# A hybrid decoder layer on one core: a narrow attention block as three fp32r matmuls, one FFN block's tiles loaded ahead, two heads' sums later

## The chip, the core and the metric

One NeuronCore of a Trainium2 chip. The time is that of the whole launch on the device in microseconds (us), the median of several runs. Five engines work side by side and meet through semaphores: TensorE (PE in the rows; its weight loads are PEld), VectorE (DVE), ScalarE (ACT), GpSimd (POOL) and SyncE (SP). SP and POOL also issue most of the DMAs, each in the order of its own queue.

## What is computed

512 tokens with 16 meta tokens ahead of them (L = 528), width 2048, one layer, all in float32. Cut to what matters:

```python
n = _rmsnorm(h, g_mix);  p = n @ w_in            # q | k | v for 8 heads of 128, and gb | gc | u
z = q @ k.T / sqrt(128)                          # q and k normed per head
log_beta, log_keep = log_sigmoid(z), where(causal, log_sigmoid(-z), 0)
log_pass = cumsum(log_keep, reverse=True) - log_keep
w = where(causal, exp(log_beta + log_pass), 0);  o_attn = w @ v
o_conv = gb * causal_dwconv3(gc * u)
h = h + concat(rmsnorm(o_attn), rmsnorm(o_conv)) @ w_out
h = h + (silu(n2 @ w_gate) * (n2 @ w_up)) @ w_down   # n2 = rmsnorm(h), hidden width 5632
```

## The kernel before

**Numbers in two parts.** Each fp32 product is made of three fp32r matmuls: a number is split into a high part (a cast to fp32r) and a low part (the number less that), and hi x hi, hi x lo and lo x hi are added in PSUM. `split` does it: `sc.copy` (ACT) writes the high part, a `tensor_tensor` (DVE) the low one. Weights stream in through SP's DMAs into `w_buf` and are split by `split_quad` (L188, L189) into `s_buf`. TensorE works through one long series of such products; everything else is fitted in between.

**The order of the work around it.** The projections go head by head: `product` runs over the 16 k tiles of the input for k (`pk`), q (`pq`) and v (`pv`). After each k tile, `tick()` counts down the pieces of work that `after(n, work)` has put on a list, and calls what is due; so `after(6, ...)` places a piece six k tiles later in the program. A scheduler then sets each engine's order from the program and its own priorities; it may move an instruction a little, as `order` rows below show. A k tile of `pk` or `pv` is six matmuls of 264 columns, one of `pq` or `pb` three of 512, one of `pcu` six of 260.

**One head's attention.** `attend` (due some k tiles after `pv`) transposes v with TensorE (L521, L522), splits it into `vh`, `vl`, and makes the logits z in three PSUM tiles. The 1344 columns of `lw`, `sp`, `lb` are the causal blocks of 128 keys: `SEG` cuts them into three segments, s = 2, 1, 0. Segment 2 holds three key blocks: 272 columns for keys 256 to 383, 144 columns for keys 384 to 511, and 16 columns for the last 16 keys. `sums(2)`, `sums(1)`, `sums(0)` (L596, L597 for s below 2) make the reverse cumulative sums with a triangular matrix; each passes the first row on to the next segment, through a one-row add (L602) and a split of that row, whose low part is the `spl` that L597 reads. Then `exp`, the causal mask (POOL, L554), and a split into `wh`, `wl`. `mix` multiplies the weights with the values into `o`: three fp32r matmuls for each of the 512, 400 and 272 columns (L621 to L623), and plain fp32 matmuls for the 144 columns (L624, values in `v32[:, :P]`) and the 16 columns (L625, 16 rows). Heads 1 to 6 have their work behind the next head's projections; head 7 has it behind the first convolution products `pcu` and `pb`.

**The FFN's input blocks.** The FFN products use seven blocks of activations for four products' worth of work (a Strassen-like scheme): `acts[0..6]`, each with a high and a low part and 8 k tiles. Blocks 3, 4 and 6 are written to DRAM (`fx`) tile by tile while the output projection runs, and loaded back at its end, when the memory of the projection's operands is free. Tile 7 is made last and written straight to SBUF. `pair_product` runs the blocks in the order 5, 0, 1, 2, 3, 4, 6 for the first pair; its matmuls are L753, and a block takes high activations with high weights, low activations with high weights, then high with low weights, 8 tiles each.

Of the kernel before, what the change touches and what calls it, by code (L numbers as in the profile page):

```python
# [9 lines left out]
F32 = mybir.dt.float32  # L10
F32R = mybir.dt.float32r
# [4 lines left out]
P = 128  # L16
D = 2048
SEQ = 512
META = 16
L = META + SEQ  # L20
HEADS = 8
# [8 lines left out]
Q0 = [0, 112, 240, 368, 496]  # L30
# [3 lines left out]
def hybrid_layer(ctx: ExitStack, tc: tile.TileContext, xT, w_in, w_out, w_gu, w_down, vecs, out):  # L34
# [10 lines left out]
    ve, sc, gp, pe = nc.vector, nc.scalar, nc.gpsimd, nc.tensor  # L45
# [108 lines left out]
    quads, sums, split_w, used, loaded = {}, {}, [], [0], [0]  # L154
# [111 lines left out]
    def after(k_tiles, work):  # L266
        waiting.append([k_tiles, work])
# [31 lines left out]
    def split(hi, lo, src, eng=ve, turn=False):  # L299
        in_order(sc.copy(hi, src), turn)  # L300
        eng.tensor_tensor(lo, src, hi.bitcast(F32), ALU.subtract)  # L301
# [187 lines left out]
    def head(h):  # L489

        if h:
            pk = pp.tile([P, 2, 512], F32, tag="pp", name=f"pk{h}")
            product([(pk[:, 0, :H], 0, H), (pk[:, 1, :H], H, L)], n_hl)
        else:
            pk = pk0
        kn = kns[0]
        kh = apool.tile([P, 384], F32R, tag="kh", name=f"kh{h}")
        kl = apool.tile([P, 384], F32R, tag="kl", name=f"kl{h}")
        after(8 if h else 11, qk_norm(halves(pk, H), g_k, L, kn[:, :L], (kh, kl, 384), f"k{h}"))

        if h:
            pq = pp.tile([P, 2, 512], F32, tag="pp", name=f"pq{h}")
            product([(pq[:, 0, :], META, L)], n_hl)
        else:
            pq = pq0
        qn = apool.tile([P, SEQ], F32, tag="qn", name=f"qn{h}")
        qh = apool.tile([P, SEQ], F32R, tag="qh", name=f"qh{h}")
        ql = apool.tile([P, SEQ], F32R, tag="ql", name=f"ql{h}")
        after(9 if h else 12, qk_norm(pq[:, 0, :], gq_s, SEQ, qn, (qh, ql, SEQ), f"q{h}"))

        pv = pp.tile([P, 2, 512], F32, tag="pp", name=f"pv{h}")
        product([(pv[:, 0, :H], 0, H), (pv[:, 1, :H], H, L)], n_hl)
        vt = t512(L, "e", 2)
        ve.tensor_tensor(two(vt[:, :L]), halves(pv, H), two(r), ALU.mult)
        after(6 if h else 11, lambda: attend(h, kn, kh, kl, qn, qh, ql, vt))

    def attend(h, kn, kh, kl, qn, qh, ql, vt):

# [1 line left out]
        for b in range(4):  # L520
            pe.transpose(ta[:, b * P : (b + 1) * P], vt[:, b * P : (b + 1) * P], ident)  # L521
        pe.transpose(tb[:16, :P], vt[:, 512:L], ident)  # L522
        vh = apool.tile([P, 384], F32R, tag="vh", name=f"vh{h}")
        vl = apool.tile([P, 384], F32R, tag="vl", name=f"vl{h}")
        v32 = apool.tile([P, 256], F32, tag="v32", name=f"v32{h}")
        split(vh, vl, ta[:, :384])
        ve.tensor_copy(v32[:, :P], ta[:, 384:512])
        ve.tensor_copy(v32[:16, P:], tb[:16, :P])


        zs = []
# [24 lines left out]
                    base=base, channel_multiplier=-1,  # L556
                )

        hl, ws = [None] * 3, [None] * 3
        for s in (2, 1, 0):  # L560
            a, b = SEG[s]
            z = zs[s][:, : b - a]
# [23 lines left out]
        def sums(s):  # L586
            a, b = SEG[s]
            th, tl = hl[s]
            c = small(f"c{h}_{s}")
            if s == 2:  # L590
                pe.matmul(c[:, :432], later_r, th, start=True, stop=False)
                pe.matmul(c[:, :432], later_r, tl, start=False, stop=False)
                pe.matmul(c[:, P:416], ones_r, bh, start=False, stop=False)
                pe.matmul(c[:, P:416], ones_r, bl, start=False, stop=True)
            else:
                pe.matmul(c[:, : b - a], carry, th, start=True, stop=False)  # L596
                pe.matmul(c[:, : b - a], carry, tl, start=False, stop=True)  # L597
            if s:

                n, (a0, b0) = SEQ - Q0[s], SEG[s - 1]  # L600
                th, tl = hl[s - 1]
                ve.tensor_tensor(lw[0:1, b0 - n : b0], c[0:1, :n], sp[0:1, a : a + n], ALU.add)  # L602
                split(th[0:1, :], tl[0:1, :], lw[0:1, a0:b0])
                after(6, lambda: sums(s - 1))
            ve.tensor_tensor(lb[:, a:b], lb[:, a:b], c[:, : b - a], ALU.subtract)
            sc.activation(lw[:, a:b], lb[:, a:b], AF.Exp)
            causal(lw, s)
            n = (512, 400, 272)[s]
            th = apool.tile([P, b - a], F32R, tag=f"th{s}", name=f"wh{h}_{s}")
            tl = apool.tile([P, b - a], F32R, tag=f"tl{s}", name=f"wl{h}_{s}")  # L610
            split(th[:, :n], tl[:, :n], lw[:, a : a + n])
            ws[s] = (th[:, :n], tl[:, :n])
            if s == 0:
                after(11, lambda: mix(ws))

        def mix(ws):
            o = small(f"o{h}")
            for b in range(3):
                kk, q0 = slice(b * P, (b + 1) * P), Q0[b]
                th, tl = ws[b]  # L620
                pe.matmul(o[:, q0:], vh[:, kk], th, start=b == 0, stop=False)  # L621
                pe.matmul(o[:, q0:], vh[:, kk], tl, start=False, stop=False)
                pe.matmul(o[:, q0:], vl[:, kk], th, start=False, stop=False)  # L623
            pe.matmul(o[:, Q0[3] :], v32[:, :P], lw[:, 1184:1328], start=False, stop=False)  # L624
            pe.matmul(o[:, Q0[4] :], v32[:16, P:], lw[:16, 1328:1344], start=False, stop=True)  # L625
            g = g_att[:, h : h + 1]
            oh, ol, store = stage_out(f"a{h}")
            sc.activation(oh, o, AF.Copy, scale=g)
            ve.scalar_tensor_tensor(ol, o, g, oh.bitcast(F32), ALU.mult, ALU.subtract)
            store()  # L630
            square_sum(acc_a, o, h == 0)
# [290 lines left out]
    for i, j in enumerate(OUT_TILES):  # L922
# [35 lines left out]
        if i == KT - 1:  # L958
            with tc.high_priority(1 << 20):
                residual(ve)  # L960
                mixed_blocks()
                square_sum(acc_h, hj, False, wide_tmp("s"), ve)
            oapool.release()
            oc2_pool.release()
            ocpool.release()
            accpool.release()
            fp = open_pool("fp")
            sides = fp.tile([P, 3 * T2], F32, name="sides")
            rings_p = {0: open_pool("ring_0")}
            pad(rings_p[0], 32)  # L970
            rings, n_ring, ring = {}, [6], {}

            groups = {0: (0, 1), 1: (1, 2), 3: (1, 1), 4: (1, 1), 5: (1, 1), 6: (2, 1), 7: (2, 5)}

            def new_places(i):
                p, m = groups[i]
                for n, t in enumerate(slots(rings_p[p], F32R, m, 6, f"ring{i}", tail=4 if i == 7 else 60, tag=f"ring{i}")):
                    ring[i + n] = t

            def ring_place():  # L980
                n_ring[0] += 1
                return ring[(n_ring[0] - 1) % 12]

            new_places(0)
            fpool_4 = open_pool("fpool_4")
            acts[4] = slot(fpool_4, F32R, 8, "f4", "f4")
            gu_pool = open_pool("gu_pool")
            gu = [gu_pool.tile([P, 2, T2], F32, name=f"gu{m}") for m in range(2)]
            pad(gu_pool, 768)
            fpool_last = open_pool("fpool_last")  # L990
            acts[3] = slot(fpool_last, F32R, 8, "f3", "f3")
            acts[6] = slot(fpool_last, F32R, 8, "f6", "f6", tail=4)
            for s, n in ((3, 6), (6, 7)):
                for part in range(2):
                    nc.sync.dma_start(acts[s][:, part, :n].bitcast(F32), fx[s][:, part, :n].bitcast(F32), max_dma_last_dim=4096)
            gp.dma_start(acts[3][:, :, 6], fx[3][:, :, 6])
            for part in range(2):
                gp.dma_start(acts[4][:, part, :7], fx[4][:, part, :7], max_dma_last_dim=4096)
            split_f(3, 6)
            split_f(4, 7)  # L1000
            split_f(6, 3)
        else:
            residual(gp if half and i < KT - 2 else ve)
            if half:
                split_f(5, 2)
                if i < KT - 2:
                    st = hbuf.tile([P, 2, 2, T2], F32R, tag="st", name=f"st{j}")[:, :, 0]
                    split(st[:, 0], st[:, 1], src[:, 3])
                    gp.dma_start(fx[6][:, :, k], st)
            else:  # L1010
                mixed_blocks()
                st = hbuf.tile([P, 2, 2, T2], F32R, tag="st", name=f"st{j}")
                split(st[:, 0], st[:, 1], src[:, 6:8])
                for n, s in enumerate((3, 4)):
                    gp.dma_start(fx[s][:, :, k], st[:, :, n])
# [241 lines left out]
```

## Time and profile before

| | |
|---|---|
| median of 3 runs | 2035.27 us (2034.88 to 2036.73) |
| the profiled execution | 2035.44 us, span 2033.7 us |
| granted TensorE clock | 1.00 |
| matmul records | 16158 |
| busy: PE, DVE, ACT, POOL | 2025.3, 1721.2, 1050.1, 382.1 us |
| HBM | 278.50 MB read, 80.61 MB written |

The timeline has a start, a duration, the engine, the line, the operation with out<-in, and in square brackets the idle time of the engine ahead of it with what ended it. Matmuls overlap, so the distance from one start to the next is what one costs. A list of waits has the waiting instruction, the one waited for, then the microseconds in total, the number of times and the longest. A plain fp32 matmul is two records, an fp32r matmul one. Rows by tile have counts and the least, median and largest duration in ns.

### The profile page before, as it was taken

What the parts mean: (1) busy time and instruction counts of PE and PEld (TensorE: products, weight loads), DVE (VectorE), ACT (ScalarE), POOL (GpSimd) and SP (SyncE); (2) the same over time, 40 slices, a digit from 0 to 9 for tenths busy, and PEclk for the clock granted to TensorE, in tenths of its full rate; (3) what the DMA queues carried; (4) which work ended last, traced back from release to release, by engine and by line L of the source; (5) the groups of instructions that cost most, each with busy time, mean ns of one, the idle gap of its engine ahead of it and who ended that gap; (6) DMA issues with size and microseconds to landing.
All of it is one profiled execution on the core that took longest, in us unless ns stands there. A gap on an engine that the chain in (4) does not pass through costs nothing.

```text
span 2033.7 us, 39736 instructions
## 1 busy us (share of the span) xinstructions
PE 2025.3 (100%) x16158; PEld 1964.0 (97%) x16158; DVE 1721.2 (85%) x2202; ACT 1050.1 (52%) x1517; POOL 382.1 (19%) x531
## 2 busy tenths in 40 slices
PE   9999999999999999999999999999999999999999
PEld 8999999999998889999999999999999999999999
DVE  8788878588877679998998998988989898888887
ACT  7666666444443435554554555555555544444443
POOL 0111111220015440111110110110110242222111
PEclk9999999999999999999999999999999999999999
DMA  6333344753365656556555555555555999989864
GB/s 231 106 125 116 124 139 133 253 153 106 104 212 181 188 173 231 167 160 181 159 160 160 160 161 158 161 161 157 164 159 156 288 322 294 244 234 265 231 149 89
DMA packets 162007, 361.70 MB, mean 178 GB/s; under 512 B 13600, under 2 KB 73760, under 8 KB 161824
## 3 DMA queue, kind: packets, MB, share of 16 engines
q1 hardware_dynamic: 79744, 229.47, 35.4%
q0 software_dynamic: 81936, 129.65, 24.3%
q8 instruction: 127, 2.08, 0.4%
q14 instruction: 56, 0.46, 0.1%
q10 hardware_dynamic: 144, 0.04, 0.0%
HBM read 278.50 MB, written 80.61 MB: 177 GB/s over the span
## 4 chain that ended last, share of the span: by engine, by line
PE 96%; DVE 1%; DMA 1%; ACT 1%; issue 0%; POOL 0%; SPq 0%; DVEq 0%; ACTq 0%
PE x L753 40%; PE z L753 20%; PE y L753 10%; PE po L859 3%; PE po L860 3%; PE po L861 3%; PE pv L286 1%; PE pv L288 1%; PE pv L290 1%; PE pk L286 1%; PE pk L288 1%; PE pk L290 1%; PE pq L290 1%; PE pq L286 1%; PE pq L288 1%; PE pcu L286 1%
## 5 line engine op out<-in xcount | busy, mean ns | idle before, releaser
L188 ACT CAST s_buf<-w_buf 128x1024 fp32r<-128x1024 f32 (+2 forms) x665 | 659.5, 992 | 755.2 <-PE x L753 368.8
L189 DVE TENSOR_TENSOR s_buf<-w_buf,s_buf 128x1024 fp32r<-128x1024 f32 (+2 forms) x665 | 767.1, 1154 | 123.3 <-ACT s_buf L188 121.4
L753 PE MATMUL x<-f,s_buf 128*128 128x256 f32 x4224 | 500.6, 275 | 1.0 <-DMA f<-fx 1.0
L753 PEld LDWEIGHTS x<-f,s_buf 128*128 128x128 f32 x4224 | 488.9, 188 | 1.3 <-DMA f<-fx 1.2
L207 DVE TENSOR_TENSOR w_buf<-w_buf 128x1024 f32<-128x1024 f32 (+1 forms) x243 | 278.3, 1145 | 16.7 <-DMA w_buf<-w_in 10.0
L753 PE MATMUL z<-f,s_buf 128*128 128x256 f32 x2112 | 253.6, 275 | 0.0
L753 PEld LDWEIGHTS z<-f,s_buf 128*128 128x128 f32 x2112 | 245.9, 188 | 0.0
L1054 POOL DMA_DIRECT2D fd<-s x147 | 103.9, 923 | 701.2 <-DVE s L301 700.0
L753 PE MATMUL x<-ring,s_buf 128*128 128x256 f32 x1824 | 219.2, 275 | 0.0
L753 PEld LDWEIGHTS x<-ring,s_buf 128*128 128x128 f32 x1824 | 212.4, 188 | 0.0
L753 PE MATMUL y<-f,s_buf 128*128 128x256 f32 x1056 | 126.8, 275 | 0.0
L753 PEld LDWEIGHTS y<-f,s_buf 128*128 128x128 f32 x1056 | 123.1, 188 | 0.1
L1127 POOL DMA_DIRECT2D out_T<-d x62 | 60.7, 1014 | 284.9 <-DVE d L1135 206.7
L753 PE MATMUL z<-ring,s_buf 128*128 128x256 f32 x864 | 105.7, 275 | 0.0
L753 PEld LDWEIGHTS z<-ring,s_buf 128*128 128x128 f32 x864 | 101.5, 188 | 0.0
L225 DVE TENSOR_TENSOR w_buf<-w_buf 128x1024 f32<-128x1024 f32 (+1 forms) x81 | 92.3, 1139 | 1.4 <-DMA w_buf<-w_down 1.4
L753 PE MATMUL x<-nh,s_buf 128*128 128x260 f32 x432 | 59.3, 282 | 0.0
L753 PEld LDWEIGHTS x<-nh,s_buf 128*128 128x128 f32 x432 | 55.0, 188 | 0.1
L789 DVE SCALAR_TENSOR_TENSOR gu<-z,sides 128x256 f32<-128x256 f32 x44 | 18.7, 425 | 42.7 <-PE z L753 42.6
L753 PE MATMUL z<-blk,s_buf 128*128 128x260 f32 x432 | 54.8, 282 | 0.0
L286 PE MATMUL pk<-nh,s_buf 128*128 128x264 f32 x256 | 52.9, 288 | 0.9 <-ACT nh L357 0.8
L753 PEld LDWEIGHTS z<-blk,s_buf 128*128 128x128 f32 x432 | 53.1, 188 | 0.0
(344 smaller groups left out, 3320.5 us busy)
## 6 DMA issues: line engine op xcount, KB each, us to landing
w_buf<-w_gu SPq DMA_DIRECT2D x176, 512.0 KB, 3.5
w_buf<-w_in SPq DMA_DIRECT2D x92, 512.0 KB, 3.4
fd<-s POOLq DMA_DIRECT2D x147, 256.0 KB, 5.2
w_buf<-w_down SPq DMA_DIRECT2D x96, 384.0 KB, 5.0
ring<-fd POOLq DMA_DIRECT2D x42, 768.0 KB, 9.2
w_buf<-w_out SPq DMA_DIRECT2D x32, 512.0 KB, 3.5
out_T<-d POOLq DMA_DIRECT2D x62, 256.0 KB, 5.5
fc<-st SPq DMA_DIRECT2D x8, 1040.0 KB, 6.1
```

The costliest lines, as they stand in the source:

```text
L188: sc.copy(hi, src)
L189: in_turn(ve.tensor_tensor(lo, src, hi.bitcast(F32), ALU.subtract), turn)
L207: in_turn(ve.tensor_tensor(sums[name], a, b, ALU.add), turn)
L225: ve.tensor_tensor(sums["t2"], sums["t2"], b["21"], ALU.add)
L286: pe.matmul(ps, wh, ah[:, a:b], start=k == 0, stop=False)
L288: pe.matmul(ps, wh, al[:, a:b], start=False, stop=False)
L290: pe.matmul(ps, wl, ah[:, a:b], start=False, stop=k == last)
L753: pe.matmul(p, wt[:, kk], act(part, k), start=first, stop=wt is lo and k == n - 1, skip_group_check=skip)
L859: pe.matmul(ps, hi[:, kk], ah, start=k == order[0], stop=False)
L860: pe.matmul(ps, hi[:, kk], al, start=False, stop=False)
L861: pe.matmul(ps, lo[:, kk], ah, start=False, stop=k == order[-1])
L1054: gp.dma_start(fd[c][s][:, :, k], t[:, :, i])
```

## The change

It has three parts. The 144 columns of segment 2 are multiplied as three fp32r matmuls: the values of all 512 keys are split, `v32` keeps only the last 16 keys, and the 144 columns of weights are split as well, one segment later, into free columns of segment 2's tiles. The loads of FFN block 4 are written ahead for its first six tiles, and tile 6 of blocks 3 and 4 comes behind them. And in heads 0 and 7 each `sums` stands seven k tiles behind the one before, not six; head 0's `attend` stands 12 behind, not 11.

```diff
-        after(6 if h else 11, lambda: attend(h, kn, kh, kl, qn, qh, ql, vt))
+        after(6 if h else 12, lambda: attend(h, kn, kh, kl, qn, qh, ql, vt))
...
-        vh = apool.tile([P, 384], F32R, tag="vh", name=f"vh{h}")
-        vl = apool.tile([P, 384], F32R, tag="vl", name=f"vl{h}")
-        v32 = apool.tile([P, 256], F32, tag="v32", name=f"v32{h}")
-        split(vh, vl, ta[:, :384])
-        ve.tensor_copy(v32[:, :P], ta[:, 384:512])
-        ve.tensor_copy(v32[:16, P:], tb[:16, :P])
+        vh = apool.tile([P, SEQ], F32R, tag="vh", name=f"vh{h}")
+        vl = apool.tile([P, SEQ], F32R, tag="vl", name=f"vl{h}")
+        v32 = apool.tile([P, P], F32, tag="v32", name=f"v32{h}")
+        split(vh, vl, ta)
+        ve.tensor_copy(v32[:16], tb[:16, :P])
...
-        hl, ws = [None] * 3, [None] * 3
+        hl, ws, late_w = [None] * 3, [None] * 3, []
...
-                after(6, lambda: sums(s - 1))
+                after(6 if 0 < h < HEADS - 1 else 7, lambda: sums(s - 1))
...
             ws[s] = (th[:, :n], tl[:, :n])
+            if s == 2:
+                late_w.extend((th[:, 272:416], tl[:, 272:416]))
+            if s == 1:
+                th, tl = late_w
+                split(th, tl, lw[:, 1184:1328])
+                ws.append((th, tl))
...
-            for b in range(3):
+            for b in range(4):
...
-            pe.matmul(o[:, Q0[3] :], v32[:, :P], lw[:, 1184:1328], start=False, stop=False)
-            pe.matmul(o[:, Q0[4] :], v32[:16, P:], lw[:16, 1328:1344], start=False, stop=True)
+            pe.matmul(o[:, Q0[4] :], v32[:16], lw[:16, 1328:1344], start=False, stop=True)
...
-            gp.dma_start(acts[3][:, :, 6], fx[3][:, :, 6])
             for part in range(2):
-                gp.dma_start(acts[4][:, part, :7], fx[4][:, part, :7], max_dma_last_dim=4096)
+                gp.dma_start(acts[4][:, part, :6], fx[4][:, part, :6], max_dma_last_dim=4096)
+            for s in (3, 4):
+                gp.dma_start(acts[s][:, :, 6], fx[s][:, :, 6])
```

What becomes of it in the engines' orders, at the places that the prediction speaks of. A row has the line, the operation, out<-in and the size of the output; numbers in names tell buffers apart, and lines after line 528 differ between the two kernels by up to 5.

The end of head 0's `mix` on TensorE, before and after (`o` is the output, `wh`, `wl` the weights, `vh`, `vl` the values, `pk` the next projection):

```order
L621 MATMUL o_1081<-wh_2_902,vh_728 128x272
L622 MATMUL o_1081<-wl_2_903,vh_728 128x272
L623 MATMUL o_1081<-wh_2_902,vl_729 128x272
L624 MATMUL o_1081<-lw_749,v_730 128x144
L625 MATMUL o_1081<-lw_749,v_730 128x16
L286 MATMUL pk_1101<-nh_170,s_buf 128x264 x2
```
```order
L626 MATMUL o_1106<-wh_2_904,vh_734 128x272
L627 MATMUL o_1106<-wl_2_905,vh_734 128x272
L628 MATMUL o_1106<-wh_2_904,vl_735 128x272
L626 MATMUL o_1106<-wh_2_904,vh_734 128x144
L627 MATMUL o_1106<-wl_2_905,vh_734 128x144
L628 MATMUL o_1106<-wh_2_904,vl_735 128x144
L629 MATMUL o_1106<-lw_754,v_736 128x16
L286 MATMUL pk_1084<-nh_208,s_buf 128x264 x2
```

One fp32 row gives way to three fp32r rows, in this head and the others; head 0's mix also stands three k tiles later, behind part of the next `pk`.

Head 0's `sums(0)` on TensorE (`c_0`), inside the product `pv` of head 1, before and after:

```order
L290 MATMUL pv_951<-nh_234,s_buf 128x264 x2
L596 MATMUL c_0_985<-sph_0_789,carry 128x512
L286 MATMUL pv_951<-nh_238,s_buf 128x264 x2
L288 MATMUL pv_951<-nl_239,s_buf 128x264 x2
L597 MATMUL c_0_985<-spl_0_790,carry 128x512
L290 MATMUL pv_951<-nh_238,s_buf 128x264 x2
```
```order
L286 MATMUL pv_937<-nh_246,s_buf 128x264 x2
L288 MATMUL pv_937<-nl_247,s_buf 128x264 x2
L290 MATMUL pv_937<-nh_246,s_buf 128x264 x2
L595 MATMUL c_0_1004<-sph_0_794,carry 128x512
L596 MATMUL c_0_1004<-spl_0_795,carry 128x512
L286 MATMUL pv_937<-nh_290,s_buf 128x264 x2
```

`nh_234` is k tile 4, `nh_238` tile 5, `nh_246` tile 7 and `nh_290` tile 8: the second matmul of `c_0` stood within the sixth tile and now stands behind the eighth. Head 7's `c_0`, before and after:

```order
L286 MATMUL pcu<-nh_358,s_buf 128x260 x2
L288 MATMUL pcu<-nl_359,s_buf 128x260 x2
L290 MATMUL pcu<-nh_358,s_buf 128x260 x2
L596 MATMUL c_0_4247<-sph_0_4032,carry 128x512
L597 MATMUL c_0_4247<-spl_0_4033,carry 128x512
L286 MATMUL pb_4264<-nh_170,s_buf 128x512
```
```order
L290 MATMUL pcu<-nh_358,s_buf 128x260 x2
L286 MATMUL pb_4276<-nh_170,s_buf 128x512
L288 MATMUL pb_4276<-nl_171,s_buf 128x512
L290 MATMUL pb_4276<-nh_170,s_buf 128x512
L286 MATMUL pb_4276<-nh_174,s_buf 128x512
L288 MATMUL pb_4276<-nl_175,s_buf 128x512
L290 MATMUL pb_4276<-nh_174,s_buf 128x512
L595 MATMUL c_0_4286<-sph_0_4052,carry 128x512
L596 MATMUL c_0_4286<-spl_0_4053,carry 128x512
```

It stood at the end of `pcu` and now stands behind two k tiles of `pb`. Last, POOL's queue at the end of the output projection, with what each DMA waits for (the DMASW names are lanes of POOL's DMAs: a DMA that waits for DMASW4 waits until the last one on lane 4 has landed):

```order
L1015 DMA fx_6637<-st_7781 256x1x256 [waits DMASW3_49,DVE_49]
L1015 DMA fx_6638<-st_7781 256x1x256 [waits DMASW4_49]
L996 DMA f_7938<-fx_6637 128x2x256 [waits DMASW5_49,DMASW3_49,PE_49]
L998 DMA f_7928<-fx_6638 128x2x896 [waits DMASW4_49,PE_49]
L998 DMA f_7928<-fx_6638 128x2x896 [waits DMASW7_49]
```
```order
L1020 DMA fx_6661<-st_7805 256x1x256 [waits DMASW3_49,DVE_49]
L1020 DMA fx_6662<-st_7805 256x1x256 [waits DMASW4_49]
L1003 DMA f_7962<-fx_6661 128x2x256 [waits DMASW5_49,DMASW3_49,PE_49]
L1001 DMA f_7952<-fx_6662 128x2x768 [waits PE_49]
L1001 DMA f_7952<-fx_6662 128x2x768 [waits DMASW7_49]
L1003 DMA f_7952<-fx_6662 128x2x256 [waits DMASW4_49,DMASW0_49]
```

The first two rows store tile 6 of blocks 3 and 4, the others load. Tile 6 of block 3 keeps its place at the head of the loads; the two large loads of block 4 lose their wait for lane 4, and a small load of tile 6 with that wait is new behind them.

## The prediction

> **What bounds the kernel.** I read the page's busy shares first, then the chain that ended last, then what TensorE waited for, then the timeline at each of those waits.
>
> ```profile
> PE 2025.3 (100%) x16158; PEld 1964.0 (97%) x16158; DVE 1721.2 (85%) x2202; ACT 1050.1 (52%) x1517; POOL 382.1 (19%) x531
> PE 96%; DVE 1%; DMA 1%; ACT 1%; issue 0%; POOL 0%; SPq 0%; DVEq 0%; ACTq 0%
> PE warm L85 <- DVE one L81: 1.1, 1, 1.1
> PE x L753 <- DMA f<-fx: 1.0, 1, 1.0
> PE pk L286 <- ACT nh L357: 0.8, 1, 0.8
> PE c L597 <- DVE spl L301: 0.6, 2, 0.3
> PE pk L288 <- DVE nl L358: 0.5, 1, 0.5
> ```
>
> TensorE is the bound from end to end: 96% of the chain is matmuls, and all its waits for other engines and DMAs come to 4.0 us (1.1 + 1.0 + 0.8 + 0.6 + 0.5). So only two kinds of edit can move the end: more or fewer TensorE microseconds, and the removal of one of those waits. Of the five rows the change touches two, the fourth FFN block (x L753 on f<-fx) and the sums (c L597); the other three lie in the start. The profiled execution took 2035.44 us (a span of 2033.7 and 1.7 around it), 0.17 above the median of 2035.27, so a term read from it can be taken off the median as it stands.
>
> **1. Mix's block of 144 columns, in 8 heads.** Matmuls overlap, so the price of one is the distance to the start of the next, not its duration. Head 1's mix, from several windows of TensorE's timeline:
>
> ```profile
> 124.36 0.29 PE L622 MATMUL o<-wl,vh 128*128 128x272 f32 x1
> 124.48 0.29 PE L623 MATMUL o<-wh,vl 128*128 128x272 f32 x1
> 124.61 0.28 PE L624 MATMUL o<-lw,v 128*128 128x144 f32 x1
> 124.73 0.28 PE L624 MATMUL o<-lw,v 128*128 128x144 f32 x1
> 124.95 0.28 PE L625 MATMUL o<-lw,v 16*128 16x16 f32 x1
> 52.30 0.60 PE L521 MATMUL va<-ident,tmp 128*128 128x128 f32 x4
> 52.74 0.27 PE L522 MATMUL vb<-ident,tmp 128*16 128x128 f32 x1
> ```
>
> The plain fp32 matmul runs as two records, 0.12 apart, and the 16-row matmul behind it starts 0.22 after the second: 0.34 us for the block (124.61 to 124.95). Of those 0.22 some 0.10 is over the 0.12 of a record; since the 16-row L625 stays, I leave that 0.10 in place. Removed: 2 records. Added: 3 fp32r matmuls of 144 columns, each with its own weights.
>
> No fp32r matmul of the trace is narrower than 256 columns, so their price is bounded. From below: 272 columns cost 0.12, and in proportion 144 cost 0.064; 3 x 0.064 + 0.10 = 0.29, 0.05 less than now. From above: if so narrow an fp32r matmul ran like the fp32 one, 0.24 each, the block would cost 3 x 0.24 + 0.10 = 0.82, 0.48 more. Between them lie the transposes L521, four matmuls of 128 columns that each load 128 columns of weights: 0.44 for four, 0.11 each, nearly the price of 272 columns. That row is nearest in width and in its loads, so I take it: 0.11 + 0.11, and for the last one 0.064 + 0.10 because the 16-row matmul has to wait for its end: 0.38, so +0.04 a head. Times 8: **+0.3 us** (ends -0.4 and +3.8).
>
> Row L521 is the evidence for a floor by weight loads. The Trainium skill, "TensorE: Matmul & The Clock Gate", section on LDWEIGHTS, has a load last as long as its column count over 1.2 GHz, whatever the rows; 107 ns for 128 columns, an estimate that agrees with the 110 ns here and speaks against this part of the change. "FP8 and Floating Point Precision", its TensorE notes, counts true FP32 as four passes; by that count alone three single passes would be a quarter cheaper than the 0.24 of today's two records, an estimate of 0.06 us a head or 0.5 us in all. The start distances decide for the first.
>
> **2. The wider splits of values and weights.** The casts, subtractions and copies that grow or go, with the nearest row for a 144-column split (that of 288 columns), and one head's busy times:
>
> ```profile
> L300 ACT CAST vh<-va x8: 479/479/480, 52.9 to 343.3; 128x384 fp32r<-128x384 f32 x8
> L301 DVE TENSOR_TENSOR vl<-va,vh x8: 539/558/559, 54.1 to 343.8; 128x384 fp32r<-128x384 f32 x8
> L527 DVE COPY v<-va x8: 272/281/281, 55.2 to 344.3; 128x128 f32<-128x128 f32 x8
> L300 ACT CAST bh<-lw x8: 428/433/433, 66.0 to 352.2; 128x288 fp32r<-128x288 f32 x8
> L301 DVE TENSOR_TENSOR bl<-lw,bh x8: 459/459/529, 67.4 to 352.7; 128x288 fp32r<-128x288 f32 x8
> 217.70:259.60 41.90, 41.90 (x288) 38.92 (x287) 33.96 (x56) 27.16 (x45) 6.75 (x15) 1.00 0.39 126
> ```
>
> ACT gains at most 0.16 (479 x 512/384 - 479) and 0.43, DVE at most 0.19 and 0.46 less the dropped copy of 0.28: some 0.6 and 0.4 a head. In the window's row DVE is busy 33.96 of a head's 41.90 us and ACT 27.16, so both have room, and heads 1 to 6 show no TensorE wait in the list. This is the cover; if it is gone, the first to wait is the next head's ss_q or z matmul, which needs a split at once. I book **+0.2** for it (0 to 2.4, third rival).
>
> **3. Sums of head 0, and its attention, later.** TensorE, then DVE:
>
> ```profile
> 75.70 0.40 PE L286 MATMUL pv<-nh,s_buf 128*128 128x264 f32 x2
> 75.94 0.40 PE L288 MATMUL pv<-nl,s_buf 128*128 128x264 f32 x2
> 76.67 0.50 PE L597 MATMUL c<-spl,carry 128*128 128x512 f32 x1 [0.33 <-DVE spl L301]
> 77.01 0.28 PE L290 MATMUL pv<-nh,s_buf 128*128 128x264 f32 x1
> 75.95 0.67 DVE L301 TENSOR_TENSOR spl<-lw,sph 1x512 fp32r<-1x512 f32 x1
> ```
>
> A pair of pv takes 0.24, so L597 was due at 76.18 and came 0.49 late, when DVE's split ended (76.62); the restart costs 0.11 more (76.67 to 77.01 is 0.34, a 512-column matmul takes 0.23). In the new order L597 stands behind eight k tiles of pv and not five and two thirds: 2.33 x 0.72 (three pairs of 0.24) = 1.7 us later, due near 77.9. DVE now has the subtraction lb - c1 (0.55) and the wider vl (0.19) ahead of this split, and c1 one k tile later (0.72 at most): 76.62 + 0.55 + 0.19 + 0.72 = 78.1 if all of it counted, and 76.6 if none did. I take **-0.5** of the 0.60 (0 to -0.6). Next late is the q norm behind it. On SP the store of the first conv blocks moves behind two more weight loads; its data is read only after the last head, so it costs nothing.
>
> **4. Sums of head 7 later.** TensorE, ACT, DVE:
>
> ```profile
> 364.83 0.41 PE L290 MATMUL pcu<-nh,s_buf 128*128 128x260 f32 x2
> 365.38 0.49 PE L596 MATMUL c<-sph,carry 128*128 128x512 f32 x1
> 366.09 0.50 PE L597 MATMUL c<-spl,carry 128*128 128x512 f32 x1 [0.22 <-DVE spl L301]
> 364.70 0.62 ACT L300 CAST sph<-lw 1x512 fp32r<-1x512 f32 x1 [1.96 <-DVE lw L602]
> 362.96 1.23 DVE L301 TENSOR_TENSOR st<-x,st 128x1040 fp32r<-128x1040 f32 x1
> 364.12 0.56 DVE L602 TENSOR_TENSOR lw<-c,sp 1x400 f32<-1x400 f32 x1
> 365.36 0.68 DVE L301 TENSOR_TENSOR spl<-lw,sph 1x512 fp32r<-1x512 f32 x1 [0.21 <-ACT sph L300]
> ```
>
> L596 was due at 365.07 and waited 0.31 for ACT's cast; L597 was due 0.23 after that and came 0.48 late; with a restart of 0.11 that is 0.90. The list's 0.3 is only the part that it counts as idle. Both now stand behind two k tiles of pb, 6 x 0.23 = 1.4 us later: L597 due near 366.7. Its split ended at 366.04. What set that was DVE's queue (L602 started as st ended), so moving c1's matmul one k tile back (to about 361.5: 365.07 less six k tiles of 0.72, plus one) does not move it; the new 144-column split stands ahead, 0.43 on ACT and 0.46 on DVE at most, so 366.04 to 366.9. I take **-0.8** (-0.9 to -0.6).
>
> **5. Loads of the fourth FFN block.** TensorE; then POOL's DMA issues, the semaphore wait ahead of the loads of block 4, and their times to landing:
>
> ```profile
> 784.80 0.61 PE L753 MATMUL x<-f,s_buf 128*128 128x256 f32 x4
> 786.43 0.74 PE L753 MATMUL x<-f,s_buf 128*128 128x256 f32 x4 [1.02 <-DMA f<-fx]
> 773.09 0.72 POOL L996 DMA_DIRECT2D f<-fx  x1 [8.34 <-PE y L753]
> 775.63 1.44 POOL L998 DMA_DIRECT2D f<-fx  x2 [1.83 <-PE x L753]
> L998 POOLq EVENT_SEMAPHORE  x1: 17/17/17, 775.1 to 775.1; - x1
> DMA to landing us min/median/max: 6.4/8.2/10.0
> ```
>
> The low parts were due at 785.25 (four matmuls of 0.11) and came at 786.43: 1.18 late, and 0.1 for the restart. The second load was issued at 775.63 + 0.72 = 776.35 and took 10.0, which gives 786.35. Both waited until 775.1 for the store of k tile 6 (DMASW4 in the order's rows, the lane of that store). In the built order block 3's tile 6 still goes first on POOL (773.09), so the six-tile loads of block 4 follow at about 773.8 and 774.5, 1.8 earlier; 774.5 + 10.0 = 784.5, in time. The small load of tile 6 keeps the wait to 775.1: with 6.4 to 10.0 it lands at 781.5 to 785.2, wanted at 785.0 (784.80 is high tile 4 of the eight, tile 6 two matmuls of 0.11 on). Behind it on POOL stand only the FFN's activation stores, which need the first gate's results, so nobody waits for it there. Taken **-1.1** (-1.3 to 0).
>
> **The sum:** 0.3 + 0.2 - 0.5 - 0.8 - 1.1 = -1.9 us, so 2035.27 - 1.9 = **2033.4 us**. Nothing hands these microseconds back, since TensorE stays the bound behind each place. 0.2% is 4.1 us, about what a measurement of this kernel can tell from no change; the forecast lies within it, and all three waits gone together (2.8) would too.
>
> **The rivals.** (a) Slower than before: narrow fp32r runs at the fp32 price. That is 0.48 x 8 = 3.8 in place of 0.3, 2033.4 + 3.5 = 2036.9. It decides the sign from 0.17 us for each of the three: 3 x 0.17 + 0.10 - 0.34 is 0.27 a head or 2.2 in all, what parts 2 to 5 bring together (2.4 - 0.2). For it, nothing in the trace is an fp32r matmul so narrow; against it, the changed program has 16166 matmul records, 8 more than the trace's 16158 (24 added, 16 gone), so each of the three is one record with one load like every other fp32r matmul, where an fp32 one is two. Chance 0.1. (b) Block 4 waits as before: the data, not the issue, was late, because SP's weight loads share the DMA engines, or tile 6 lands last. 2033.4 + 1.1 = 2034.5; chance 0.12. (c) The added casts make a new wait in each head, 0.3 us (half of ACT's 0.6): 2.4 in place of 0.2, 2035.6; for it, spl follows ACT's cast directly in parts 3 and 4; against it, the room in part 2. Chance 0.08. The low end of the main case is all gains whole, no cast felt and mix at its lower bound: 2035.27 - 0.6 - 0.9 - 1.3 - 0.4 = 2032.1.
>
> **Numbers.** The main case has 0.66 (2032.1 to 2034.3), (b) 0.12, (c) 0.08, (a) 0.1, what I don't see 0.04. The range 2032.0 to 2035.6 holds the main case, (b) and half of (c) and more. Below 2031.2 (faster by over 0.2%) I see no case, as the waits touched don't suffice: 0.03. Above 2039.3: (a) and (c) together reach only 2039.1: 0.02. Within: 0.95.
>
> **What the next profile would show.** Mix: three starts some 0.11 apart and L629 0.16 after the last; starts 0.24 apart mean (a). The list of waits without the row for c and without that for f<-fx; L753's gap near 784 gone. If the f row stays near 1.0, (b). New rows of 0.2 or more for ss_q or z mean (c). I am wrong if the time is above 2035.6, or if these rows vanish and the time does not fall.

## The result and the profile after

The changed kernel took **2039.7 us** (median of 10 runs, 2038.6 to 2046.8) where the kernel before, on the same chip, took 2034.6 (2034.1 to 2036.7): a ratio of 1.0029 [1.0021, 1.0037], 5.1 us slower. The forecast was 2033.4, with a range to 2035.6. The profiled execution took 2038.66 us, one of the shortest of the ten, so its trace shows a little less than the median difference.

From the page: busy time by engine, and the chain that ended last, by engine. Then the list of waits of TensorE (us in total, times, longest).

```profile
PE 2027.7 (100%) x16166; PEld 1965.9 (97%) x16166; DVE 1717.5 (84%) x2202; ACT 1053.0 (52%) x1525; POOL 387.6 (19%) x532
PE 90%; ACT 3%; DVE 3%; issue 2%; POOL 1%; DMA 0%; SPq 0%; POOLq 0%; DVEq 0%; ACTq 0%
PE ss_q L474 <- ACT sh_q L300: 2.1, 6, 0.9
PE warm L85 <- DVE one L81: 1.1, 1, 1.1
PE ss_q L475 <- DVE sl_q L301: 1.1, 5, 0.2
PE pk L288 <- DVE nl L358: 0.4, 1, 0.4
PE pk L286 <- ACT nh L357: 0.2, 1, 0.2
PE z L535 <- ACT qh L300: 0.2, 1, 0.2
```

The two rows that the change was to remove (c and f<-fx) are gone. In their place stand two rows for `ss_q`, the sums over the q norm's squares: TensorE waits there in head 1 and in heads 3 to 7. TensorE's share of the chain fell from 96% to 90%; ACT and DVE have 3% each for 1%, and POOL 1%. The list counts only the idle part; by the distances of starts each of the five waits of heads 3 to 7 costs 0.9 to 1.1 us (at 206 us: 0.43 late at L474, 0.50 at L475 and 0.10 for the restart), and the one of head 1 some 1.1: 6.2 us in all. The kernel before loses some 0.16 us at the same place in heads 3 to 6 (the last three rows of its block below), which its list does not show; against it the six waits cost 5.6.

What comes before such a wait, in head 4, whose `ss_q` stands at 206 us. Timeline of the changed kernel (start, duration, engine, line), first DVE, then POOL, ACT and PE:

```profile
198.12 0.29 DVE L301 TENSOR_TENSOR wl<-lw,wh 128x144 fp32r<-128x144 f32 x1
198.46 0.68 DVE L301 TENSOR_TENSOR spl<-lw,sph 1x512 fp32r<-1x512 f32 x1
199.07 0.69 DVE L309 TENSOR_TENSOR tmp<-tmp 128x528 f32<-128x528 f32 x1
199.69 0.41 DVE L435 SCALAR_TENSOR_TENSOR x<-x 128x260 f32<-128x260 f32 x1
200.03 0.69 DVE L310 TENSOR_TENSOR tmp<-tmp,tmp 128x528 f32<-128x528 f32 x1
201.47 0.58 DVE L301 TENSOR_TENSOR wl<-lw,wh 128x400 fp32r<-128x400 f32 x1 [0.75 <-ACT wh L300]
199.53 1.35 POOL L553 TENSOR_SCALAR_AFFINE_SELECT lw<-lw 128x128 f32<-128x128 f32 x1 [4.68 <-ACT lw L605]
200.91 0.53 ACT L300 CAST wh<-lw 128x400 fp32r<-128x400 f32 x1 [1.51 <-POOL lw L553]
205.88 0.62 ACT L300 CAST sh_q<-tmp 128x512 fp32r<-128x512 f32 x1
206.55 0.50 PE L474 MATMUL ss_q<-sh_q,ones_r 128*128 128x512 f32 x1 [0.27 <-ACT sh_q L300]
207.28 0.50 PE L475 MATMUL ss_q<-sl_q,ones_r 128*128 128x512 f32 x1 [0.23 <-DVE sl_q L301]
```

The same place in the kernel before:

```profile
196.82 0.41 DVE L435 SCALAR_TENSOR_TENSOR x<-x 128x260 f32<-128x260 f32 x1
197.17 0.68 DVE L301 TENSOR_TENSOR spl<-lw,sph 1x512 fp32r<-1x512 f32 x1
197.78 0.69 DVE L309 TENSOR_TENSOR tmp<-tmp 128x528 f32<-128x528 f32 x1
198.50 0.71 DVE L310 TENSOR_TENSOR tmp<-tmp,tmp 128x528 f32<-128x528 f32 x1
198.23 0.39 POOL L554 TENSOR_SCALAR_AFFINE_SELECT lw<-lw 128x128 f32<-128x128 f32 x1 [4.69 <-ACT lw L606]
198.66 0.53 ACT L300 CAST wh<-lw 128x400 fp32r<-128x400 f32 x1 [0.55 <-POOL lw L554]
203.63 0.62 ACT L300 CAST sh_q<-tmp 128x512 fp32r<-128x512 f32 x1
204.74 0.39 PE L474 MATMUL ss_q<-sh_q,ones_r 128*128 128x512 f32 x1
205.03 0.51 PE L475 MATMUL ss_q<-sl_q,ones_r 128*128 128x512 f32 x1
205.37 0.40 PE L286 MATMUL pv<-nh,s_buf 128*128 128x264 f32 x2
```

L309 is the k norm's square in `rsqrt`, L310 the product that needs its result, L435 the last step of `form_blocks`. Before, L310 starts 0.72 us after L309, where back to back it would be 0.61 (197.17 to 197.78): VectorE stands still for 0.11 us until its own result is there. POOL's causal select of segment 1 (L554, in the changed kernel L553) is done just there and takes 0.39 us. In the changed kernel the new 144-column subtraction has taken L435's old place, and L435 has moved between L309 and L310. VectorE now runs from 198.46 to 200.72 without a stop, and the select ends only at 200.88, after 1.35 us. ACT's cast `wh` waits for the select (1.51 idle for 0.55). From the start of L309 to the start of that cast it is 0.88 before (197.78 to 198.66) and 1.84 after. `sh_q`, behind it on ACT, is late by the same 0.96 and had 0.49 of room (it ended at 204.25, L474 came at 204.74). L475, behind the low part `sl_q` on VectorE, had no room at all: before the change it came 0.29 us after L474, where 0.23 is the distance without a wait, and the row behind it 0.34 after that.

From this theory T: the moved L435 closes a gap in VectorE's queue, GpSimd's select starves, ACT is late, TensorE waits. Rival R1: the added casts and subtractions as such make ACT and VectorE late, whatever their order. Rival R2: the later sums of head 0 shift all heads that follow.

### The profile page after: what moved, and what is told of

Same layout as the page of the kernel before. It is cut to its first block, busy times and chain, and to the rows that moved or that the text cites. A ratio compares the mean times of both kernels' runs of the same rounds, so it can differ in the third digit from the quotient of the medians.

```text
span 2037.0 us, 39762 instructions
## 1 busy us (share of the span) xinstructions
PE 2027.7 (100%) x16166; PEld 1965.9 (97%) x16166; DVE 1717.5 (84%) x2202; ACT 1053.0 (52%) x1525; POOL 387.6 (19%) x532
## 4 chain that ended last, share of the span: by engine, by line
PE 90%; ACT 3%; DVE 3%; issue 2%; POOL 1%; DMA 0%; SPq 0%; POOLq 0%; DVEq 0%; ACTq 0%
PE x L757 40%; PE z L757 20%; PE y L757 10%; PE po L864 3%; PE po L863 3%; PE po L865 3%; PE pcu L286 1%; PE pcu L288 1%; PE pcu L290 1%; DVE s_buf L189 1%; POOL lw L553 1%; PE pv L286 1%; PE pq L288 1%; PE pq L290 1%; PE pq L286 1%
## 5 line engine op out<-in xcount | busy, mean ns | idle before, releaser
L286 PE MATMUL pv<-nh,s_buf 128*128 128x264 f32 x256 | 53.1, 288 | 0.0
```

What stands on the lines that cost most here:

```text
L286: pe.matmul(ps, wh, ah[:, a:b], start=k == 0, stop=False)
```

## Experiments

Each time is a median in us, with the range, beside runs of the kernel before on the same chip (its medians in the four groups were 2034.32, 2034.36, 2034.41 and 2034.06, of 18 to 33 runs). The ratio is to that kernel; runs of different groups are compared below by their differences to it.

| run | kernel | us (range, runs) | ratio [95%] |
|---|---|---|---|
| e1 | before + mix | 2041.43 (2041.2 to 2042.1, 5) | 1.0034 [1.0021, 1.0047] |
| e2 | after without mix | 2034.51 (2033.4 to 2038.8, 11) | 1.0000 [0.9991, 1.0009] |
| e3 | after, 144-column split early | 2036.42 (2035.7 to 2037.2, 11) | 1.0009 [1.0001, 1.0018] |
| e4 | after, segment 1's mask on VectorE | 2032.91 (2032.0 to 2035.6, 11) | 0.9994 [0.9985, 1.0003] |
| e5 | before, gap filled | 2039.79 (2039.0 to 2040.6, 7) | 1.0028 [1.0017, 1.0038] |
| e6 | before, same instruction elsewhere | 2035.33 (2034.9 to 2036.6, 11) | 1.0005 [0.9997, 1.0014] |
| e7 | before + new loads | 2036.63 (2033.9 to 2039.5, 11) | 1.0009 [1.0000, 1.0018] |
| e8 | sums, loads, mask on VectorE | 2034.42 (2033.2 to 2040.5, 11) | 1.0008 [1.0000, 1.0017] |
| e9 | before + later sums | 2032.81 (2032.5 to 2035.6, 11) | 0.9993 [0.9984, 1.0001] |
| e10 | mix, sums, mask on VectorE | 2032.78 (2032.1 to 2034.3, 11) | 0.9991 [0.9982, 1.0000] |
| e11 | sums, mask on VectorE | 2034.11 (2033.3 to 2034.9, 11) | 0.9997 [0.9988, 1.0006] |
| e12 | before, mask on VectorE | 2035.15 (2034.7 to 2036.7, 11) | 1.0004 [0.9995, 1.0013] |
| e13 | mix, sums (after, old loads) | 2039.46 (2038.4 to 2040.2, 8) | 1.0025 [1.0015, 1.0036] |
| e14 | as e7 | 2036.30 (2033.2 to 2038.4, 11) | 1.0007 [0.9998, 1.0017] |

**e1 and e2: the mix part alone, and everything but it.** e1 takes the hunks of `vh`/`vl`/`v32`, of `late_w` and of `mix` into the kernel before; e2 takes the same hunks out of the changed kernel.

> The kernel before with the mix part alone (144 columns as three fp32r matmuls, their split, the wider value split); loads and sums as before. Theory T (the added 144-column subtraction pushes the convolution form block's last step between the k norm's square and the product that waits for it; that closes VectorE's gap there, GpSimd's select of segment 1's weights lasts 1.35 us for 0.39, ScalarE's cast behind it and with it the q norm's squares are late): this order stands in six heads here, so six waits at ss_q of about 1.0 us, +6.3 us, about 2040.9. Rival R1 (the added cast and subtraction as such make ScalarE and VectorE late, whatever the order): the same +5 to +6. Rival R2 (the sums of head 0 moved by a k tile shift every later head): no waits at ss_q here, +0.3 us, about 2034.9.

> The changed kernel without the mix part: later sums of heads 0 and 7 and the FFN loads alone. T and R1: selects of segment 1 at 0.39 us, no waits at ss_q in heads 3 to 7, the gains of the other parts stay (0.6 + 0.9 + 1.2 us by the waits that are gone): 2032.0, and up to 1 us more if the wait in head 1 belongs to the later sums. R2: the waits stay, 2037 to 2039.

e1 is 7.1 us slower than before with the sums untouched: R2 falls. L435 stands between L309 and L310 in six heads here, and the list has the waits of six heads (against five in the changed kernel, where head 1's is another, below):

```profile
PE ss_q L475 <- DVE sl_q L301: 1.4, 6, 0.2
PE ss_q L474 <- ACT sh_q L300: 1.2, 4, 0.4
```

e2 has no `ss_q` row, and its selects of segment 1 in those heads last 0.39 us (0.48 in one). Its time however is that of the kernel before, and not 2032: something in the two other parts gave back what the sums brought (e7, e9).

**e3: the same instructions in another order.** The 144-column cast and subtraction get a priority that puts them ahead of the 272-column ones; L435 then falls back to its old place.

```diff
-                split(th, tl, lw[:, 1184:1328])
+                with tc.high_priority(1 << 20):
+                    split(th, tl, lw[:, 1184:1328])
```

> The changed kernel with the 144-column cast and subtraction at a high priority: the same instructions, but VectorE does this subtraction ahead of the 272-column one, and the form block's last step stands ahead of the k norm's square again, as before the change. T: segment 1's selects back at 0.39 us, the five ss_q waits of heads 3 to 7 gone, after minus 5: about 2034.6. R1: the load is the same, 2039 to 2040.

Timeline of DVE, POOL and PE at the same place:

```profile
198.94 0.69 DVE L309 TENSOR_TENSOR tmp<-tmp 128x528 f32<-128x528 f32 x1
199.66 0.71 DVE L310 TENSOR_TENSOR tmp<-tmp,tmp 128x528 f32<-128x528 f32 x1
199.40 0.39 POOL L553 TENSOR_SCALAR_AFFINE_SELECT lw<-lw 128x128 f32<-128x128 f32 x1 [5.03 <-ACT lw L605]
205.92 0.39 PE L474 MATMUL ss_q<-sh_q,ones_r 128*128 128x512 f32 x1
206.18 0.50 PE L475 MATMUL ss_q<-sl_q,ones_r 128*128 128x512 f32 x1
```

The gap is open (0.72 between the starts), the select takes 0.39, and all five waits of heads 3 to 7 are gone, with every instruction of the change still there: R1 cannot explain that. The loss fell by 3.0 us (from 5.1 to 2.1) and not by 5. Head 1's wait stayed (1.0 in the list), and the early split brought its own: TensorE is 0.4 to 0.5 late at a `c` in heads 2, 3 and 7.

**e4: GpSimd out of the chain.** `seen` is a constant tile with ones where the select keeps a value.

```diff
-            causal(lw, s)
+            if s == 1:
+                ve.tensor_tensor(lw[:, a : a + P], lw[:, a : a + P], seen, ALU.mult)
+            else:
+                causal(lw, s)
```

> The changed kernel with the causal mask of segment 1's weights made by VectorE, as a product with a 128x128 tile of ones and zeros, not by a GpSimd select. T: GpSimd is out of that chain, the five ss_q waits are gone, about 2034.6 to 2035. R1: VectorE has one instruction more in each head (some 0.2 us), the waits grow: 2040 to 2042.

The product takes the gap (0.27 us from 197.95, between the square and its product), the cast follows at 198.31:

```profile
197.95 0.27 DVE L613 TENSOR_TENSOR lw<-lw,seen 128x128 f32<-128x128 f32 x1
198.31 0.53 ACT L306 CAST wh<-lw 128x400 fp32r<-128x400 f32 x1 [0.65 <-DVE lw L613]
```

No `ss_q` row is left, head 1's neither, and the time is 2032.9: by the differences 6.5 below the changed kernel, although VectorE does one instruction more in each head. R1 expected 2040 or more. T expected 2034.6 to 2035, since it left head 1's wait in place.

**e5 and e6: the gap alone, without any part of the change.** One instruction with the shape of L435 that nothing reads, put into the kernel before: in e5 between L309 and L310, in e6 behind the norm's last product (there with `dst` in place of `y`).

```diff
         eng.tensor_tensor(t[:, :n], y[:, :n], y[:, :n], ALU.mult)
+        if fill:
+            ve.scalar_tensor_tensor(gap, y[:, :260], -1.0, y[:, 260:520], ALU.mult, ALU.subtract)
         eng.tensor_tensor(t[:, :n], t[:, :n], v, ALU.mult)
```

> The kernel before with one instruction more on VectorE in the k norms of heads 2 to 7: a scalar_tensor_tensor of 128x260 with the shape and the two SBUF operands of the form block's last step, into a tile that nothing reads, between the norm's square and the product that waits for it. Nothing else moves. T: the gap is closed, segment 1's selects take 1.3 us for 0.39 in six heads, the q norm's sums wait some 1.0 us in each, so 2034.3 plus 6: about 2040. R1 (VectorE's added time alone): 0.41 us more in six heads with 84% of VectorE busy, at most 0.2 to 0.4 us of wait in each, 2035 to 2036.5.

> The same added instruction in the same six heads, but behind the k norm's last product; the gap between the norm's square and the product stays open. T: selects stay at 0.39 us; the instruction stands ahead of the q norm's low part, so up to 0.3 us a head can show as a wait for that: 2034.3 to 2036. R1: as the run with the filled gap, within 0.5 us of it.

e5, timeline of DVE, POOL and PE (its L311 is the square, L314 the product, L478 the first sum):

```profile
199.56 0.69 DVE L311 TENSOR_TENSOR tmp<-tmp 128x528 f32<-128x528 f32 x1
200.18 0.41 DVE L313 SCALAR_TENSOR_TENSOR gap<-tmp 128x260 f32<-128x260 f32 x1
200.52 0.69 DVE L314 TENSOR_TENSOR tmp<-tmp,tmp 128x528 f32<-128x528 f32 x1
200.02 1.35 POOL L559 TENSOR_SCALAR_AFFINE_SELECT lw<-lw 128x128 f32<-128x128 f32 x1 [4.68 <-ACT lw L611]
207.04 0.50 PE L478 MATMUL ss_q<-sh_q,ones_r 128*128 128x512 f32 x1 [0.32 <-ACT sh_q L300]
```

and e6 (L311 and L312 the same two):

```profile
197.83 0.69 DVE L311 TENSOR_TENSOR tmp<-tmp 128x528 f32<-128x528 f32 x1
198.56 0.71 DVE L312 TENSOR_TENSOR tmp<-tmp,tmp 128x528 f32<-128x528 f32 x1
198.29 0.39 POOL L559 TENSOR_SCALAR_AFFINE_SELECT lw<-lw 128x128 f32<-128x128 f32 x1 [4.68 <-ACT lw L611]
```

All six selects last 1.35 us in e5 and 0.39 in e6. The same instruction costs 5.4 us in the gap and 1.0 beside it. 0.41 us of VectorE in six heads is 2.5 us of work; the gap that it fills, six times 0.11, was worth 4.5 us. With e3 and e4 this shows T.

**e7, e14, e8: the loads.**

> The kernel before with the FFN loads alone moved. If the 1.0 us wait for the fourth FFN block in the profile before stands in every run, it goes: 2033.2. If it is one of several DMA waits that come and go from run to run (the profiles of other kernels show waits of 0.5 to 1.0 us in other places, one of them at this block with the new loads): no change, 2034.3.

> The later sums and the FFN loads, no mix part, and segment 1's mask as a VectorE product. T: what the mask run gave (2032.9) less the mix's 0.3 us and its splits: 2032.4 to 2032.9, below the kernel before. R1: 2034.5 as without the mask, or more, since VectorE has more to do.

> The FFN loads alone once more, the same kernel as in e7. If a late transfer of tile 6 is this order's own: again some runs 3 to 5 us above the others, none of the kernel before, and a median above 2034.4. If e7 met a disturbance: 2033.2 to 2034.4 in all runs but one or two.

Alone, the new loads made the median 2.3 and 2.2 us longer, not 1.1 shorter: five of e7's eleven runs lie at 2037.2 or above and six of e14's at 2036.3 or above, the others at 2033.2 to 2036.6. Of e8's eleven, five lie at 2037.7 to 2040.5; the same kernel with the old loads (e11) has none above 2034.9. The kernel before was once above 2036.4 in its 107 runs beside these. e7's profiled execution is one of the long ones (2039.45). PE, the loads on POOL (the two of block 4 and the last one of tile 6), the landing times of L999 (both loads of tile 6), and in the DMA view from 786 to 788 us the two queues, q1 with the weight loads and q0 with POOL's (packets, MB, share of 16 engines):

```profile
783.96 0.84 PE L753 MATMUL x<-f,s_buf 128*128 128x256 f32 x6
788.45 0.80 PE L753 MATMUL x<-f,s_buf 128*128 128x256 f32 x2 [3.65 <-DMA f<-fx]
773.06 1.45 POOL L997 DMA_DIRECT2D f<-fx  x2
774.88 0.71 POOL L999 DMA_DIRECT2D f<-fx  x1 [0.38 <-issue]
DMA to landing us min/median/max: 7.5/10.5/13.5
q1 hardware_dynamic: 22, 0.07, 9.5%
q0 software_dynamic: 10, 0.01, 1.9%
```

The separate load of tile 6, issued at 774.88, landed 13.5 us later, at 788.4, and TensorE, which wanted it at about 784.6, went on at 788.45. In e2's execution the same two loads took 5.6 and 7.5 us, and in e14's, which is one of its short ones (2033.83), 5.4 and 7.9. In the last two microseconds the DMA engines were nearly idle and POOL's queue moved ten packets, so weight loads in its way do not explain that end. That the other long runs are of this kind is not shown, since no other was profiled. Why such a load is late in some runs only, and seldom in the other kernels that have it (one of e2's eleven runs is above 2036, none of e3 or e4 above 2037.3, two of ten of the changed kernel above 2042), stays open.

**e9 to e13: the sums alone, and combinations with the old loads.**

> The kernel before with the later sums of heads 0 and 7 alone. By the prediction's terms -0.5 and -0.8: 2033.0. By the attention stage of the run without the mix part (0.4 us ahead of before at its end, start excluded, with two new waits at c of 0.4 to 0.5 us): 2033.9. No run above 2037.5, since the FFN loads are the old ones.

> The mix part and the later sums with segment 1's mask as a VectorE product, and the FFN loads as before. T and the reading that the new loads only add a late transfer in some runs: 2032.9 as with the new loads, no run above 2036. If the new loads do gain 1 us: 2034.

> The later sums and the VectorE mask, no mix part, FFN loads as before. If the late runs of e8 (five of eleven above 2037) come from the new loads, they are gone here and the median is that of its other runs, 2033.2 to 2034; against the run with the mix part this gives the mix's own price with GpSimd out of the chain: 0.3 us less by the prediction.

> The kernel before with segment 1's mask as a VectorE product alone. T: its selects there last 0.39 us and hold up nothing in heads 2 to 7, so nothing to gain beside the shorter chain to the cast: 2033.8 to 2034.4. If GpSimd's part in the chain was already a bound before the change: 2032 to 2033.

> The changed kernel with the FFN loads as before (mix part and later sums stay). T: 2032.8 of the sums alone, plus five ss_q waits of 1.0, the 1.0 in head 1 and 0.3 of the mix: 2039.1, no run above 2041. If the new loads are part of the loss: as much below the changed kernel's 2039.7 as they cost it, 0.5 to 2 us; if they gain 1.1 us as predicted: 2040.8.

The sums bring 1.6 us (e9), its profile has no row for `c`, and no run lies above 2035.6. The changed kernel with the old loads (e13) is at 2039.46, so the loads' share in the changed kernel is nothing that these runs can tell. The mask on VectorE is no gain of its own (e12, 0.7 longer): it pays only where the gap is closed. e11 without the mix part is 1.3 us longer than e10 with it, so the mix's own price of 0.3 does not show against what each new order does; that difference was not followed up. e9 and e10 are the shortest, 1.6 us below the kernel before and 6.7 below the changed one by the differences; their intervals reach to 1.0001 and 1.0000, so that a gain over the kernel before is not certain.

## Why the prediction was wrong

The account in differences to the kernel before: sums -1.6 (e9); with the mix part +5.4 (e13), so +7.0 for it, as in e1 (+7.1); with the loads +5.1, so about -0.3 for these here. The traces of e9 and e13 differ by the mix part alone. From head 0's `ss_q` to the `pv` row behind head 7's, the one takes 289.7 us and the other 295.9, 6.1 more; by the distances of starts the waits at `ss_q` cost 5.7 more and the mix 0.04 in each of six heads, together 5.9. So in that stretch the loss is these waits and little else; the 0.9 us between its 6.1 and the medians' 7.0 is within their intervals.

- **Part 1, the 144 columns (+0.3): right in the sum, by luck in its terms.** Head 1's mix after has start distances of 0.07, 0.11 and 0.20, together 0.38 us for 0.34 before. The prediction had 0.11, 0.11 and 0.16: the first is below the 0.11 that it took as a floor, the last above its term, and the two errors cancel. Rival (a) is out.

```profile
124.68 0.23 PE L626 MATMUL o<-wh,vh 128*128 128x144 f32 x1
124.75 0.27 PE L627 MATMUL o<-wl,vh 128*128 128x144 f32 x1
124.86 0.27 PE L628 MATMUL o<-wh,vl 128*128 128x144 f32 x1
125.06 0.39 PE L629 MATMUL o<-lw,v 16*128 16x16 f32 x2
```

- **Part 2, the wider splits (+0.2, at most 2.4): the step that failed.** "So both have room" was read from busy time (33.96 and 27.16 of 41.90 us). The place was right: `ss_q` was named as the first to wait, and rival (c) had such a wait, at 0.3 us a head. The size and the mechanism were not: it costs about 1.0 a head, and it is not the 0.4 us that VectorE does more but the order in which the scheduler put the new subtraction and L435. The selects of GpSimd, which is 19% busy, have no part in the prediction. The second support, "heads 1 to 6 show no TensorE wait in the list", was no cover either: by the start distances of the trace before, L475 already came late in heads 3 to 6, for 0.16 us a head. That trace also had selects of one shape that took 0.30 us with nothing behind them on VectorE and 0.39 in the gap. A time above 2039.3 had a chance of 0.02, because the prediction knew of nothing beyond (a) and (c) together, 2039.1.
- **Head 1's wait (1.1)** is in the changed kernel, e3 and e13, and not in e1, e2 or e9: it needs the later sums and the mix part together. The changed kernel's trace shows the same mechanism with other neighbours (POOL, then ACT):

```profile
76.23 1.03 POOL L553 TENSOR_SCALAR_AFFINE_SELECT lw<-lw 128x128 f32<-128x128 f32 x1 [5.02 <-ACT lw L605]
77.28 0.53 ACT L300 CAST wh<-lw 128x400 fp32r<-128x400 f32 x1 [1.19 <-POOL lw L553]
```

  Head 0's select of segment 1 ends at 77.26, behind a series on VectorE that ends at 77.09; ACT idles 1.19 us for it, and `sh_q` stands behind this cast on ACT; in e9 it stands ahead of it. In e4 and e10, without the select, the wait is gone.
- **Parts 3 and 4, the sums (-1.3): right**, 1.6 measured (e9, whose interval reaches to no gain), and the rows for `c` are gone in e9, e13 and the changed kernel.
- **Part 5, the loads (-1.1): wrong.** The step that failed took the 1.0 us wait for f from one execution as a cost of every run. Eight other kernels have the old loads (e1, e5, e6, e9 to e13), and no list of theirs has such a row. And the small load of tile 6 was given 6.4 to 10.0 us to land; in e7's execution it took 13.5.

## What to carry over

A busy share of 84% does not say that an engine has room: ask which gaps in its queue another engine lives on, and look at what a scheduler puts into them when an instruction is added. Where GpSimd shares a chain with VectorE, print VectorE's order around each GpSimd instruction, before and after, and look for dependent pairs that have been pulled apart. A list of waits leaves small ones out: read the room at a place from the distances of starts. A DMA wait seen in one profiled execution is one draw; take it off the time only if a second execution shows it.

## What the runs showed of the hardware

A GpSimd select of 128x128 took 0.30 us in head 7, where VectorE had nothing to do from 0.15 us after its start (the row below, POOL's timeline of the kernel before), 0.39 when VectorE stood still for 0.11 us between two dependent instructions, and 1.35 when three VectorE instructions followed one another without that stop (0.69, 0.41 and 0.69 us); moving one instruction switched between the last two. In all these rows, and in those of e3, e5, e6 and of head 0 above, the select ends 0.15 to 0.17 us after the end of the VectorE instruction at which the series stopped (in head 4 at 198.62 for 198.47 before, at 200.88 for 200.72 after).

```profile
365.89 0.30 POOL L554 TENSOR_SCALAR_AFFINE_SELECT lw<-lw 128x128 f32<-128x128 f32 x1 [5.11 <-ACT lw L606]
```

The Trainium skill, "SBUF — State Buffer", section "Who interferes with whom", says that a VectorE instruction with two SBUF inputs contends with a GpSimd instruction that reads SBUF, and that the port pair which they share is an exclusive lock. The rows agree on the place (L309, L435 and L310 read SBUF twice), and show more than that: the select stayed unfinished not for one instruction but until the whole series had ended, over two boundaries between instructions (199.69 and 200.03). That this port pair is the reason is what the Trainium skill says; no run here separates it from another one.

That such a place is worth 4.5 us of 2034 by the order alone (e5 against e6) was more than the whole change was forecast to move.
